# Moving one bank copy ahead, keeping the last gated chunks on the chip, and moving the residual loads to GpSimd's queue, in a float32 gated block

## The chip, the cores and the metric

The kernel runs on one core of one Trainium2 chip. The core has five engines that work in parallel: TensorE (PE: matmuls, into PSUM banks of 128 x 512 float32), VectorE (DVE), ScalarE (ACT), GpSimd (POOL) and SyncE (SP), which here only issues DMAs. SP, ACT and POOL each issue DMAs on a queue of their own. Each engine runs its instructions in order and waits on semaphores for the others. The metric is the time of one execution on the device in microseconds (us).

## The reference

A residual block on x of 1024 tokens by 1024 channels, in float32. Its second half is a gated feed-forward layer, and its first step is one wide input projection:

```python
h = rms_norm(x, norm_mix_g[l]) * (1.0 + sc1) + sh1
proj = jnp.einsum('bsd,de->bse', h, w_in[l])          # 7 x 1024 columns
...
x = x + g1 * mix
h2 = rms_norm(x, norm_ffn_g[l]) * (1.0 + sc2) + sh2
a, bgate = jnp.split(jnp.einsum('bsd,df->bsf', h2, w_ffn_in[l]), 2, axis=-1)
x = x + g2 * jnp.einsum('bsf,fd->bsd', jax.nn.silu(a) * bgate, w_ffn_out[l])   # 2816 hidden channels
return rms_norm(x, final_norm_g)
```

Between them lie two convolution mixers, their projections and a gated merge, which the change does not touch.

## The kernel before

Everything is held transposed, channels on the 128 partitions and tokens along the free axis, so x is 8 tiles of 128 x 1024 and the hidden layer 22 chunks (f = 0 to 21). Tokens are used in two halves of 512, which is one PSUM bank.

**Matmuls.** A float32 operand is split in a high part (a cast on ScalarE: `wh`, `th`) and a low part (the difference, on VectorE or GpSimd: `wl`, `tl`). `mm3` multiplies them in three matmuls: wh by th (L323), wh by tl (L324), wl by th (L326). A row "L324 x<-tl,wh" is thus the second matmul of a triple into a bank of x, and it needs the low part.

**Duals and products.** Matrix products are done in pairs of column blocks, called duals, by a scheme with seven products in place of eight, named "1", "2", "6", "5", "7", "3", "4" in the order they run. Sums of blocks of the weights (L243 to L245, L259, on 128 x 1024 or 128 x 768 tiles called `raw`) are made beforehand. "1", "6", "7" and "4" use the two banks x (one for each of the two column blocks, p = 0 and 1), "2" the banks y, "5" and "3" the banks z. A product that uses a bank again adds to what stands in it, and may start only when the intermediate sum has been read. A product of an input dual has 2 x 4 triples, one of an output dual 2 x 3.

**Run-ahead.** For the first duals of the input projection the products "1" and "2" are computed early, while the normalisation of the second token half is still being made. Their results are kept in tiles `m1`. `win_dual` (L760) copies `m1` back into the two banks x at the head of each such dual, and "6" then adds to them. The loop `steps` (L637 on) is the last part of the run-ahead; its last pass computes product "2" of the last of these duals.

**Feed-forward input.** Eleven duals (d = 0 to 10) make two hidden chunks each. `hid_set(d)` prepares them as operands: for d = 0 to 8 the seven combinations that the output duals use, for d = 9 and 10 (chunks 18 to 21, from `REST` on) the plain chunks. `store` splits a tile into a high and a low half in one of three buffers called `stage`, and GpSimd's queue writes it to DRAM (L1166, 512 KB). `t_load` (L1192) reads it back in two halves of 256 KB, `th` and `tl`, into tiles of a pool of 58.

**Feed-forward output.** Three groups g of three pairs of chunks, in two duals d of the output channels each: (0,0), (0,1), (1,0) and so on. `product` runs the seven products, and after each `out_evac` (L1263) adds the bank to the residual tiles x1 (x10 to x17) in place on VectorE: "1", "2", "6" and "3" to x10 and x11 in dual d = 0 (x12 and x13 in d = 1), "5", "7" and "4" to x14 and x15 (x16 and x17). x10 and x11 are loaded early; the other six are loads of 512 KB on SP's queue (L1256), in the order 4, 5, 2, 3, 6, 7, into a pool `x1b` opened when the pools `gi` and `stage` are closed, in their memory. The products of a group are loaded one group ahead. Chunks 18 to 21 are multiplied last, in pieces of tokens, followed by the final normalisation.

**What sets the order.** The program is written in one sequence; a scheduler with its own simulated times orders each engine's instructions, and pools of buffers add waits. `tc.issue_after(ins)` keeps what is issued under it behind `ins` on the same engine only. GpSimd's DMAs use eight semaphores in turn, so each waits until the one eight before it has landed.

Of the kernel before, what the change touches and what calls it, by code (L numbers as in the profile page):

```python
# [45 lines left out]
FC = DFF // P  # L46
# [59 lines left out]
REST = 2 * GROUP * GROUPS  # L106
# [9 lines left out]
def block_kernel(ctx: ExitStack, tc: tile.TileContext, xt, x0, xT, c, vecs, ada, w_first, w_duals,  # L116
# [522 lines left out]
    for i, (d, m) in enumerate(steps):  # L639
        if 0 < i <= KH:  # L640
            h1_pair(i - 1)
        w = next_w()
        for p in range(d == LEAD // 2, 2):
            if m == "1":
                ahead[d, p] = ps_tile("ahead")
            for k in range(KH):
                c0 = ((p * KH if d > LEAD // 2 else 0) + k) * P
                mm3([ahead[d, p]], slice(c0, c0 + P), w, [th[m][k]], m == "1" and k == 0, k == KH - 1, m == "2")
            (m1_store if m == "1" else first_out)(d, p, ahead[d, p])
        if i == 0:  # L650
            with tc.issue_after(mm3.ins):
                rx_1 = row_sum(spread)
# [60 lines left out]
    def win_dual(d, pairs, x, y, z):  # L713
# [44 lines left out]
        if d < AHEAD_DUALS:  # L758
            for p in range(2):
                nc.scalar.copy(x[p], m1[d, p])  # L760
# [121 lines left out]
    n_duals = len(PAIRS) // 2  # L882
    banks = [[ps_tile(b) for _ in range(2)] for b in "xyz"]
    for d in range(n_duals):
# [273 lines left out]

    hid_dram = {}

# [7 lines left out]
    def hid_set(d):  # L1168

        (b11, b12), (b21, b22) = ((ha[2 * d + p, "4"], ha[2 * d + p, "6"]) for p in range(2))  # L1170
        if 2 * d >= REST:
            for p, half in enumerate(((b11, b12), (b21, b22))):
                for h in range(2):
                    store((2 * d + p, h), half[h])
            return
# [78 lines left out]
    x1 += [x1bp.tile([P, T], F32, tag="x1", name=f"x1{j}") for j in range(2, KC)]  # L1254
    for j in (4, 5, 2, 3, 6, 7):
        nc.sync.dma_start(x1[j], x1_dram[j])  # L1256

# [9 lines left out]

    hid = {}
    n = 2 * GROUP * P
# [4 lines left out]
    for g in range(GROUPS):  # L1274
        for d in range(2):
            banks = {}
            for m in PRODUCTS:
                product(banks, m, to[g, m], out_evac(d))
                if d == 0 and m == "1":
                    if g < GROUPS - 1:  # L1280
                        for q in PRODUCTS:
                            group_load(g + 1, q)
                    else:
                        for h in range(2):
                            for f in range(REST, FC):
                                hid[f, h] = t_load((f, h))
# [166 lines left out]
```

## Time and profile before

| | |
|---|---|
| median of 3 runs | 1468.57 us (1468.46 to 1469.9) |
| the profiled execution | 1469.82 us |
| its span, first to last instruction | 1468.0 us |
| mean granted clock of TensorE | 0.996 |
| DMA | 262.98 MB, mean 179 GB/s |

The profile is of one execution. A row of the waits reads: engine, what it waited to do, the line, what released it, total us, times, longest. A row of a timeline reads: start, us, engine, line, operation, tile written <- tiles read, count, and in brackets the idle time before it and what ended that. A row of the windows gives the stretch, then for PE, PEld, DVE, ACT and POOL the busy time with the number of instructions, then the granted clock, the share of DMA and GB/s. SPq is SyncE's queue of DMA issues. The last number of a DMA row is the median time from issue to landing.

The input projection's first dual starts near 88 us. The last feed-forward input dual ends and the output phase begins near 1236 us.

### The profile page before, as it was taken

To read this page: it belongs to the slowest core of one execution; us is meant where nothing else is said; L and a number is where in the kernel's file an instruction comes from. 1 tells how busy PE (TensorE), PEld (TensorE's weight loads), DVE (VectorE), ACT (ScalarE), POOL (GpSimd) and SP (SyncE) were. 2 spreads that over 40 slices of the span, in tenths; PEclk is the share of its full clock that TensorE was granted. 3 is DMA by queue.
4 is the path that set the end of the run, shared out by engine and by line. 5 is a ranking of instruction groups with operands and counts; after the bars stand their busy time and mean duration, and the time that the engine had idled before them with its cause. 6 is when DMAs were issued, how large, how long until landed. Compare 5 with 4: busy or idle time off the path is not lost.

```text
span 1468.0 us, 17816 instructions
## 1 busy us (share of the span) xinstructions
PE 1447.8 (99%) x6393; PEld 1188.4 (81%) x6393; DVE 1167.9 (80%) x1604; ACT 652.7 (44%) x959; POOL 527.4 (36%) x466
## 2 busy tenths in 40 slices
PE   8999999999999999999999999999999999999997
PEld 4778888888888888888888888888888888788887
DVE  6898899999989959999677897677776665676755
ACT  4874443433333446465236565444444443122235
POOL 0028788768777762111022002001011025435105
PEclk9999999999999999999999999999999999999999
DMA  9943554231322346576485348454554459998403
GB/s 380 363 157 117 178 158 129 87 129 59 128 86 73 113 145 220 196 231 204 147 287 187 104 155 274 143 181 167 171 178 148 144 176 375 343 282 269 143 22 115
DMA packets 90618, 262.98 MB, mean 179 GB/s; under 512 B 10401, under 2 KB 12577, under 8 KB 90530
## 3 DMA queue, kind: packets, MB, share of 16 engines
q1 hardware_dynamic: 45952, 149.97, 30.7%
q0 software_dynamic: 37232, 96.49, 20.1%
q10 hardware_dynamic: 7346, 15.40, 2.8%
q8 instruction: 50, 0.82, 0.2%
q14 instruction: 38, 0.31, 0.1%
HBM read 198.90 MB, written 62.91 MB: 178 GB/s over the span
## 4 chain that ended last, share of the span: by engine, by line
PE 51%; issue 4%; DVE 2%; DMA 1%; POOL 1%; ACT 0%; POOLq 0%; DVEq 0%; SPq 0%
PE x L323 8%; PE x L324 8%; PE x L326 8%; PE z L323 4%; PE z L326 4%; PE z L324 4%; PE y L323 3%; PE y L326 3%; PE y L324 3%; PE mix L323 2%; PE mix L326 2%; PE mix L324 2%; PE yb L323 1%; PE yb L324 1%; PE yb L326 1%
## 5 line engine op out<-in xcount | busy, mean ns | idle before, releaser
L220 ACT CAST wh<-raw 128x1024 fp32r<-128x1024 f32 (+3 forms) x262 | 264.6, 1011 | 412.2 <-PE x L324 117.1
L221 DVE TENSOR_TENSOR wl<-raw,wh 128x1024 fp32r<-128x1024 f32 (+2 forms) x180 | 208.5, 1160 | 75.6 <-ACT wh L220 74.2
L221 POOL TENSOR_TENSOR wl<-raw,wh 128x1024 fp32r<-128x1024 f32 x82 | 202.0, 2469 | 90.2 <-ACT wh L220 90.2
L821 DVE SCALAR_TENSOR_TENSOR c<-diff,vec,c 128x512 f32<-128x512 f32 x248 | 179.0, 750 | 2.7
L1166 POOL DMA_DIRECT2D hid<-stage x71 | 37.8, 533 | 336.8 <-DVE stage L364 333.9
L324 PE MATMUL x<-tl,wh 128*128 128x512 f32 x304 | 118.6, 390 | 0.6 <-DVE tl L364 0.6
L323 PE MATMUL x<-th,wh 128*128 128x512 f32 x304 | 118.5, 390 | 0.0
L326 PE MATMUL x<-th,wl 128*128 128x512 f32 x304 | 118.3, 389 | 0.0
L323 PE MATMUL z<-th,wh 128*128 128x512 f32 x216 | 84.6, 392 | 2.1 <-DVE x L1263 2.1
L821 DVE SCALAR_TENSOR_TENSOR c<-u,wsum,c 128x512 f32<-128x512 f32 x112 | 84.1, 751 | 2.0
L326 PE MATMUL z<-th,wl 128*128 128x512 f32 x216 | 84.5, 391 | 0.0
L324 PE MATMUL z<-tl,wh 128*128 128x512 f32 x216 | 84.5, 391 | 0.0
L326 PE MATMUL y<-th,wl 128*128 128x512 f32 x180 | 70.1, 390 | 0.2 <-POOL wl L221 0.2
L324 PE MATMUL y<-tl,wh 128*128 128x512 f32 x180 | 70.0, 389 | 0.0
L323 PE MATMUL y<-th,wh 128*128 128x512 f32 x180 | 70.0, 389 | 0.0
L364 DVE TENSOR_TENSOR stage<-g,stage 128x512 fp32r<-128x512 f32 x62 | 41.9, 688 | 34.5 <-ACT stage L363 34.5
L243 POOL TENSOR_TENSOR raw<-raw 128x1024 f32<-128x1024 f32 x13 | 33.6, 2582 | 95.3 <-DVE t2l L364 78.9
L324 PEld LDWEIGHTS x<-tl,wh 128*128 128x128 f32 x304 | 57.2, 188 | 12.9 <-DVE tl L364 1.0
L323 PEld LDWEIGHTS x<-th,wh 128*128 128x128 f32 x304 | 57.2, 188 | 12.0
L326 PEld LDWEIGHTS x<-th,wl 128*128 128x128 f32 x304 | 57.2, 188 | 11.8
L1192 POOL DMA_DIRECT2D th<-hid x71 | 38.2, 538 | 75.2 <-PE x L326 56.6
L363 ACT CAST stage<-g 128x512 fp32r<-128x512 f32 x62 | 37.4, 619 | 51.8 <-DMA hid<-stage 43.5
(759 smaller groups left out, 4023.4 us busy)
## 6 DMA issues: line engine op xcount, KB each, us to landing
hid<-stage POOLq DMA_DIRECT2D x71, 512.0 KB, 5.2
raw<-in_w_duals SPq DMA_DIRECT2D x66, 512.0 KB, 3.6
raw<-in_w_fi SPq DMA_DIRECT2D x53, 512.0 KB, 4.6
th<-hid POOLq DMA_DIRECT2D x71, 256.0 KB, 5.7
tl<-hid POOLq DMA_DIRECT2D x71, 256.0 KB, 5.8
ada<-in_ada SPq DMA_DIRECT2D x33, 512.0 KB, 6.0
raw<-in_w_fo SPq DMA_DIRECT2D x24, 384.0 KB, 6.5
raw<-in_w_conf SPq DMA_DIRECT2D x16, 512.0 KB, 4.3
```

Of the source, the lines that this page charges most:

```text
L220: hi = nc.scalar.copy(wh, raw)
L221: lo = lo_engine.tensor_tensor(wl, raw, f32(wh), ALU.subtract)
L243: eng.tensor_tensor(a["s1"], a["21"], a["22"], ALU.add)
L323: nc.tensor.matmul(ps, wh, xh, start=first, stop=False, skip_group_check=again)
L324: nc.tensor.matmul(ps, wh, xl, start=False, stop=False, skip_group_check=again)
L326: mm3.ins = nc.tensor.matmul(ps, wl, xh, start=False, stop=last, skip_group_check=again).ins
L363: nc.scalar.copy(hi, src)
L364: t_split.ins = nc.vector.tensor_tensor(lo, src, f32(hi), ALU.subtract).ins
L821: tap.ins = nc.vector.scalar_tensor_tensor(out=out, in0=src[:, s : s + H], scalar=wt, in1=acc, op0=ALU.mult, op1=ALU.add).ins
L1166: nc.gpsimd.dma_start(hid_dram[key], s)
L1192: nc.gpsimd.dma_start(t, hid_dram[key][:, s])
```

## The change

It has two parts.

**The copy.** The copy of the first dual's first bank from `m1[0, 0]` is no longer made at the head of `win_dual`; it is issued in the last pass of `steps`, ahead of that pass's matmuls, into a bank taken there. The second bank is copied where it was.

**The last chunks and the residual.** For the last input dual (chunks 20 and 21) `hid_set` splits straight into tiles of the pool of 58 (`hid`), which stay until the end; they are neither stored nor loaded again. Chunks 18 and 19 go by DRAM as before. The six residual loads are issued on GpSimd's queue, in two calls: x14 and x15 where the six stood, the other four after the first output product.

```diff
         w = next_w()
+        if i == len(steps) - 1:
+            first_x = [ps_tile("x")]
+            nc.scalar.copy(first_x[0], m1[0, 0])
         for p in range(d == LEAD // 2, 2):
...
         if d < AHEAD_DUALS:
-            for p in range(2):
+            for p in range(d == 0, 2):
                 nc.scalar.copy(x[p], m1[d, p])
...
-    banks = [[ps_tile(b) for _ in range(2)] for b in "xyz"]
+    banks = [first_x + [ps_tile("x")]] + [[ps_tile(b) for _ in range(2)] for b in "yz"]
...
-    hid_dram = {}
+    hid_dram, hid = {}, {}
...
                 for h in range(2):
-                    store((2 * d + p, h), half[h])
+                    if d < N_IN - 1:
+                        store((2 * d + p, h), half[h])
+                    else:
+                        hid[2 * d + p, h] = t_pair("hid")
+                        t_split(half[h], *hid[2 * d + p, h])
...
-    for j in (4, 5, 2, 3, 6, 7):
-        nc.sync.dma_start(x1[j], x1_dram[j])
+
+    def x1_load(js):
+        for j in js:
+            nc.gpsimd.dma_start(x1[j], x1_dram[j])
+
+    x1_load((4, 5))
...
                 product(banks, m, to[g, m], out_evac(d))
+                if (g, d, m) == (0, 0, "1"):
+                    with tc.issue_after(mm3.ins):
+                        x1_load((2, 3, 6, 7))
...
-                            for f in range(REST, FC):
+                            for f in range(REST, FC - 2):
                                 hid[f, h] = t_load((f, h))
```

The scheduler's order changes in three places.

ScalarE at the end of the run-ahead, before and after. `x_915` (after: `x_808`) is the first bank x of the first dual, `x_916` (`x_917`) the second; `ahead` are the run-ahead's banks, `th` the high parts of the operands for "5" and "7".

```order
L582 COPY p2_820<-ahead_689 128x512
L363 CAST th_838<-x00_213 128x512
L586 ACTIVATE sig_835<-ahead_706 128x512
L760 COPY x_915<-m1_332 128x512
L587 DMA gate_a0_118<-sig_835 128x512
L363 CAST th_842<-x10_227 128x512
L760 COPY x_916<-m1_337 128x512
```

```order
L645 COPY x_808<-m1_332 128x512
L582 COPY p2_822<-ahead_689 128x512
L586 ACTIVATE sig_837<-ahead_706 128x512
L363 CAST th_840<-x00_213 128x512
L587 DMA gate_a0_118<-sig_837 128x512
L363 CAST th_844<-x10_227 128x512
L763 COPY x_917<-m1_337 128x512
```

The first copy has moved ahead of three instructions, the second stands where it was. On TensorE the three matmuls of "5" that read `th_840` and `tl_841` now stand between the two halves of "6".

VectorE some 10 us further on, before and after. `wl_963` is the low part of the weights of product "3"; `tl_859`, `tl_863`, `tl_867` (after: `tl_861`, `tl_865`, `tl_869`) are low parts of the second, third and fourth chunk of product "7".

```order
L364 TENSOR_TENSOR tl_859<-x11_497,th_858 128x512
L364 TENSOR_TENSOR tl_863<-x21_499,th_862 128x512
L221 TENSOR_TENSOR wl_963<-raw_959,wh_962 128x1024
L364 TENSOR_TENSOR tl_867<-x31_501,th_866 128x512
L364 TENSOR_TENSOR tl_871<-x41_503,th_870 128x512
```

```order
L364 TENSOR_TENSOR tl_861<-x11_497,th_860 128x512
L221 TENSOR_TENSOR wl_963<-raw_959,wh_962 128x1024
L364 TENSOR_TENSOR tl_865<-x21_499,th_864 128x512
L364 TENSOR_TENSOR tl_869<-x31_501,th_868 128x512
L364 TENSOR_TENSOR tl_873<-x41_503,th_872 128x512
```

The weights' split has moved ahead of the third chunk's. ScalarE's casts for it moved in the same way: the second bank's copy `v_953` and the cast `wh_962` stand one or two places sooner.

GpSimd's queue at the start of the output phase, before and after. `hid20_0` to `hid21_1` are the stores that go away, `hid3_1` and so on the loads of the second group, `x14` to `x17` and `x12`, `x13` the residual.

```order
L1192 DMA tl_9883<-hid2_4_7658 128x512
L1166 DMA hid20_0_9889<-stage_9886 128x1024
L1166 DMA hid20_1_9894<-stage_9891 128x1024
L1166 DMA hid21_0_9899<-stage_9896 128x1024
L1192 DMA th_9977<-hid3_1_7908 128x512
L1166 DMA hid21_1_9904<-stage_9901 128x1024
L1192 DMA tl_9978<-hid3_1_7908 128x512
L1192 DMA th_9981<-hid4_1_8193 128x512
```

```order
L1199 DMA tl_9883<-hid2_4_7658 128x512
L1199 DMA th_9973<-hid3_1_7908 128x512
L1265 DMA x14_9917<-x1_dram4_5925 128x1024
L1265 DMA x15_9918<-x1_dram5_5926 128x1024
L1265 DMA x12_9915<-x1_dram2_5923 128x1024
L1265 DMA x13_9916<-x1_dram3_5924 128x1024
L1265 DMA x16_9919<-x1_dram6_5927 128x1024
L1265 DMA x17_9920<-x1_dram7_5928 128x1024
L1199 DMA tl_9974<-hid3_1_7908 128x512
```

The stores are gone, and all six residual loads stand together, one place behind the first store's old place: `issue_after` a matmul holds nothing back on GpSimd.

VectorE in the first output dual, after, where the additions of "5" and "7" to x14 and x15 stand. `z` holds "5", `x` holds "7"; `wl_10135` is the low part of the weights of "4"; `raw_10162` is a block of the weights of dual (0,1).

```order
L221 TENSOR_TENSOR wl_10109<-raw_9925,wh_10108 128x768
L1274 SCALAR_TENSOR_TENSOR x14_9917<-z_10112,ng2_9902,x14_9917 128x512
L1274 SCALAR_TENSOR_TENSOR x15_9918<-z_10123,ng2_9902,x15_9918 128x512
L221 TENSOR_TENSOR wl_10135<-raw_9929,wh_10134 128x768
L243 TENSOR_TENSOR raw_10214<-raw_10162,raw_10164 128x768
L1274 SCALAR_TENSOR_TENSOR x14_9917<-x_9947,ng2_9902,x14_9917 128x512
L244 TENSOR_TENSOR raw_10162<-raw_10162,raw_10158 128x768
L1274 SCALAR_TENSOR_TENSOR x15_9918<-x_9958,ng2_9902,x15_9918 128x512
```

Before, the three sums L243 to L245 stood six instructions later, behind the next dual's first two weights. SP issues the load of `raw_10162` when `wl_10109` is done; before, the corresponding load stood behind the six residual loads.

More of the change, by code (lines that the diff above doesn't have):

```diff
@@ L1266, in out_evac @@
         return evac
-    hid = {}
     n = 2 * GROUP * P
```

## The prediction

> **What bounds the kernel now.** I read the page's engine shares first, then the waits of TensorE, then the two places where the change acts. Times are us from the span's start.
>
> ```profile
> PE 1447.8 (99%) x6393; PEld 1188.4 (81%) x6393; DVE 1167.9 (80%) x1604; ACT 652.7 (44%) x959; POOL 527.4 (36%) x466
> PE z L323 <- DVE x L1263: 2.1, 1, 2.1
> ...
> PE x L323 <- ACT x L760: 1.4, 1, 1.4
> ...
> PE x L324 <- DVE tl L364: 0.6, 1, 0.6
> ```
>
> TensorE is busy for 99% of the span, so an edit can only win back a stall of TensorE. The first two waits are the two that the change aims at; the third lies 14 us behind the second and is fed by the same engines.
>
> The larger one stands in the output phase. Four windows of equal length, and TensorE's events around the stall:
>
> ```profile
> 1200.00:1240.00 40.00, 40.00 (x178) 33.15 (x177) 22.44 (x28) 16.18 (x25) 24.05 (x46) 1.00 1.08 338
> 1240.00:1280.00 40.00, 37.87 (x160) 30.81 (x160) 23.87 (x32) 7.80 (x10) 16.77 (x33) 0.96 1.06 351
> ...
> 1257.95 0.39 PE L326 MATMUL z<-th,wl 128*128 128x512 f32 x1
> 1260.47 0.50 PE L323 MATMUL z<-th,wh 128*128 128x512 f32 x1 [2.13 <-DVE x L1263]
> ...
> 1263.38 0.63 PE L326 MATMUL z<-th,wl 128*128 128x512 f32 x1
> 1263.80 0.63 PE L323 MATMUL x<-th,wh 128*128 128x512 f32 x1
> ...
> 1262.00:1263.00 1.00, 1.00 (x4) 0.71 (x4) 1.00 (x2) 0.00 (x0) 0.00 (x0) 0.50 1.11 399
> ```
>
> The second window holds 160 matmuls where the first holds 178. At 40 / 178 = 0.225 us each, 18 missing ones are 4.05 us. Only 2.3 us of that is the gap (1258.18, one step after the last matmul, to 1260.47); the rest is the slow stretch behind it, in which the granted clock is 0.50 and matmuls start 0.42 us apart instead of 0.227.
>
> What TensorE waited for:
>
> ```profile
> SPq L1256 <- DMA hid<-stage: 8.2, 1, 8.2
> ...
> 1253.29 6.25 DMA x<-x_dram
> 1259.66 0.76 DVE x L1263
> ```
>
> The bank of product "3", second half, still held product "5"; VectorE could not add it to x15 because x15 had not landed. Its load stood in SP's queue for 8.2 us behind the landing of a store from the stage buffers, whose memory x15 takes over.
>
> The second place is the start of the first dual:
>
> ```profile
> 87.78 0.39 PE L326 MATMUL ahead<-h70h,wl 128*128 128x512 f32 x1
> 89.58 0.50 PE L323 MATMUL x<-t2h,wh 128*128 128x512 f32 x1 [1.42 <-ACT x L760]
> ...
> 86.50 1.04 ACT L220 CAST wh<-raw 128x1024 fp32r<-128x1024 f32 x1
> ...
> 88.92 0.60 ACT L760 COPY x<-m 128x512 f32<-128x512 f32 x1
> ```
>
> The next slot was 88.01, the matmul came at 89.58: 1.57 us lost, on a ScalarE copy that stood behind three others.
>
> **Part B, the on-chip hidden chunks and the residual loads.** Removed: four stores of 512 KB, eight loads of 256 KB, and the wait of x15 for a store's landing. The four splits write other tiles at the same price: no change on ScalarE or VectorE, except that the ScalarE split which waited for a stage buffer does not wait. Moved: six loads of 512 KB from SP's queue to GpSimd's, where they stand one place behind the old place of the first store:
>
> ```profile
> 1239.13 0.54 POOL L1166 DMA_DIRECT2D hid<-stage  x1 [0.15 <-issue]
> 1239.81 1.17 POOL L1166 DMA_DIRECT2D hid<-stage  x2
> ...
> hid<-stage POOLq DMA_DIRECT2D x2, 512.0 KB, 8.0
> th<-hid POOLq DMA_DIRECT2D x9, 256.0 KB, 8.3
> ```
>
> x14 and x15 now take the slots 1239.81 and about 1240.45. The two stores issued there, of the same size on the same queue, landed after 8.0 us at the median. So I put x14 and x15 at about 1248 and 1249. They are wanted by 1255.4 (x14, to be added before the first half of product "3", which starts nine matmuls, 2.04 us, before 1258.18) and by 1257.4 (x15). That is over 7 us to spare, and the stall goes: -4.05. The other four loads are wanted from 1266 on and issued by 1243. Beyond 1257.4 each us late costs one, and at 1259.6, 19 us after issue, nothing is gained. Ends: 0 and -4.05; the row is far nearer to the second.
>
> What is late next? Two things.
>
> First, VectorE's queue: the sum L243 of the next weights now stands behind `wl_10135` and ahead of the second addition to x14. It waits for `raw_10162`, which SP issues when `wl_10109` is done:
>
> ```profile
> 1249.59 0.95 DVE L221 TENSOR_TENSOR wl<-raw,wh 128x768 fp32r<-128x768 f32 x1
> ...
> raw<-in_w_fo SPq DMA_DIRECT2D x24, 384.0 KB, 6.5
> ...
> raw<-in_w_fo SPq DMA_DIRECT2D x2, 384.0 KB, 14.5
> ```
>
> Issue 1250.5, landing 6.5 later at 1257.0, sum 0.95, addition 0.75: the bank is free at 1258.7. Product "4" wants it at 1258.18 + 2.04 = 1260.2. Slack 1.5 us, so I take 0 for it. The other end is the 14.5 us of the second row, seen when that load stood behind five residual loads in SP's own queue: free at 1266.7, a stall of 6.5 us. Now the residual loads are on the other queue and mostly landed by 1252, so the median is the nearer row.
>
> Second, the eight tiles that keep the hidden chunks leave 50 of 58 for the streamed loads, so loads for the second group wait until the second dual of the first group frees tiles, from about 1266. They are read from about 1293 (seven products of 18 matmuls from 1264.3). With 8.3 us for a load, nothing there reaches TensorE; 0. GpSimd issues no arithmetic in this phase, so nothing but these loads is queued behind its waits.
>
> **Part A, the copy.** x[0] is now copied in front of the `p2` copy, behind the cast that ends at 87.54: 87.44 to 88.03, and TensorE starts at 88.09, 1.49 us sooner. The copies and casts it passes are each 0.6 later by that, and still ahead of their readers. The lead does not last. The order puts the first three matmuls of product "5" ahead of the second half of "6". Twelve matmuls from 88.09 end the first half at 90.9; the next but one wants a low part that VectorE ends at 91.26 (first of the three from 90.59) and waits 0.2. Fifteen more matmuls start by 94.5: "6" ends near 94.65, 0.67 sooner than before (95.31, where ScalarE's copy `v` follows at 95.35). The 21 left of "5" bring "7" to 99.24, where it was 100.59. It wants the low parts of its third and fourth chunk seven and ten matmuls later, at 100.83 and 101.5. They come so:
>
> ```profile
> 97.27 2.41 POOL L244 TENSOR_TENSOR raw<-raw 128x1024 f32<-128x1024 f32 x1 [12.37 <-DMA raw<-in_w_duals]
> 99.76 3.27 POOL L245 TENSOR_TENSOR raw<-raw 128x1024 f32<-128x1024 f32 x1
> ...
> 90.59 1.88 DVE L364 TENSOR_TENSOR tl<-x,th 128x512 fp32r<-128x512 f32 x3
> 92.39 1.21 DVE L221 TENSOR_TENSOR wl<-raw,wh 128x1024 fp32r<-128x1024 f32 x1
> ...
> 96.49 0.69 DVE L364 TENSOR_TENSOR tl<-x,th 128x512 fp32r<-128x512 f32 x1 [1.08 <-ACT th L363]
> 97.44 3.33 DVE L221 TENSOR_TENSOR wl<-raw,wh 128x1024 fp32r<-128x1024 f32 x1 [0.26 <-ACT wh L220]
> 100.68 4.11 DVE L364 TENSOR_TENSOR tl<-x,th 128x512 fp32r<-128x512 f32 x3
> ...
> 95.35 0.59 ACT L772 COPY v<-x 128x512 f32<-128x512 f32 x1 [1.10 <-PE x L326]
> ...
> 96.35 1.05 ACT L220 CAST wh<-raw 128x1024 fp32r<-128x1024 f32 x1
> ...
> 103.64 0.50 PE L324 MATMUL x<-tl,wh 128*128 128x512 f32 x1 [0.62 <-DVE tl L364]
> ```
>
> A split that takes 1.21 took 3.33 while GpSimd's sum ran, and of the three behind it (0.69 when free) the first took 2.9: the two engines shut each other out. After the change the third chunk's `tl_865` stands behind `wl_963`, not ahead of it. ScalarE's chain of v, th and wh (2.05 us, 95.35 to 97.40 before) now runs from 94.68, so `wl_963` starts at 96.78; GpSimd's data lands at 97.27 as before, so it waits for the split's end at 98.0. [...]
>
> If GpSimd goes first: sum to 100.4, `tl_865` done at 100.9 (0.1 late), second sum to 103.2, `tl_869` done at 103.75. TensorE goes on at 103.79 against 103.64 before: all 1.49 us are gone, +0.15. If VectorE goes first, both low parts are there by 101.5, and up to 103.64 - 101.5 = 2.1 us stay; a sum of GpSimd's then falls among the splits for product "3" and may take 0.9 of it back (-1.2 to -2.1, middle -1.6). The rows lean to the first:
>
> ```profile
> 531.09 2.84 POOL L259 TENSOR_TENSOR raw<-raw 128x1024 f32<-128x1024 f32 x1
> 533.89 2.84 POOL L221 TENSOR_TENSOR wl<-raw,wh 128x1024 fp32r<-128x1024 f32 x1
> ...
> 531.60 6.29 DVE L710 TENSOR_TENSOR q<-sc,q 128x512 f32<-128x512 f32 x3
> ...
> 80.94 3.96 POOL L243 TENSOR_TENSOR raw<-raw 128x1024 f32<-128x1024 f32 x1 [78.94 <-DVE t2l L364]
> ...
> 81.97 0.68 DVE L627 TENSOR_TENSOR x<-x,x 128x512 f32<-128x512 f32 x1
> ```
>
> At 99.76, 531.09 and 533.89 GpSimd was waiting and went ahead of the next VectorE instruction; at 80.94 it waited, and VectorE's next, at 81.97, still went first. I take +0.15, between ends of -2.1 and +1.9 (below).
>
> [...]
>
> **Sum.** -4.05 + 0.15 = -3.9. On the profiled execution's 1469.82 that is 1465.9. That execution stands 1.25 above the median of the three runs, 1468.57, and the comparison is of medians: 1464.7.
>
> **The rivals.**
> [...]
> - The new stall of "7" is a gap of 2.1 us, as long as the one at 1260.47, and brings the slow clock with it: 1.75 more (4.05 - 2.3). For it: that row. Against: the 1.42 gap at 89.58 had no slow matmuls behind it, and 2.13 is the shortest here that did. -4.05 + 1.9 = -2.15, so 1466.4.
> - Part B doesn't do what it says: x14 or x15 lands late, behind eight outstanding loads with the queues at 351 GB/s, and half of the stall stays. For it: the loads of 10 us and more around 1255. Against: even 14.5 us would be in time. -2 + 0.15 = -1.85, so 1466.7.
> - The slow stretch from 1261 on is not brought by the gap and stays when the gap closes. For it: the 1.42 gap had no such stretch. Against: no other stretch of 1240 to 1280 is slow, and this one follows the gap. -2.3 + 0.15 = -2.15, again 1466.4. [...]
> - Slower: `raw_10162` lands late and VectorE, in order, holds the additions behind L243. Above a landing at 1258.5 each us costs one, and a gap of 2 us brings the slow clock's 1.75. It ends over 0.2% slower from a stall of 5.1 us on, a landing at 1263.6, 13.1 us after issue. For it: the 14.5 row, which gives -4.05 + 6.5 + 1.75 + 0.15 = +4.35, so 1472.9. Against: it stood behind five loads then.
>
> **How the numbers follow.** 0.2% is 2.9 us, about what a measurement of this kernel can tell from no change: faster is below 1465.6, slower above 1471.5. Chances: forecast 0.29, VectorE first 0.21, slow clock in "7" 0.19, half stall 0.14, slow stretch stays 0.05, late L243 0.12 (0.10 of it slower, 0.02 same). Faster 0.29 + 0.21 = 0.50, slower 0.10, same 0.40. The range goes from 1462.4 (VectorE first at its end of -2.1) to 1468.6, which takes in the half stall together with the slow clock in "7" (-2 + 1.9); it leaves out the late L243 and little below. The forecast with VectorE first, the faster cases alone, is 1462.4 to 1465.5.
>
> **What the profile after would show.** TensorE's wait on DVE x in the output phase gone, and 178 matmuls in 1240 to 1280; x14 and x15 landed by 1250; no TensorE wait on L1274 near 1260. In the first dual TensorE's x at 88.1 without the ScalarE wait, and in its place a wait of L324 on `tl` of about 2 us near 101.6, with GpSimd's L244 starting its work as VectorE's `wl` ends. The prediction is wrong if `wl` and both `tl` run back to back there, if the clock falls behind that wait, or if L243 stands idle on a load beyond 1258.5.

## The result, and the profile after

The changed kernel takes 1467.20 us at the median of 20 runs (1464.4 to 1469.39); the kernel before, run beside it, takes 1470.14 (20 runs, 1467.77 to 1474.14). That is 2.94 us less, a ratio of 0.998 with a 95% interval of 0.9973 to 0.9987. It is faster by about the 0.2% that a measurement of this kernel can tell from no change. The prediction had a saving of 3.9 us and put it against a median of three runs, 1468.57, which lay 1.57 below the later one.

The profiled execution of after took 1468.79 us (span 1467.0, mean granted clock 0.996), so it is only 1.0 shorter than the one before, and that 1.0 is a sum of terms of both signs. TensorE's longest waits, in the view of the waits of the changed kernel:

```profile
PE x L324 <- DVE tl L364: 1.8, 1, 1.8
PE lead L485 <- POOL idle L478: 1.7, 1, 1.7
PE lead L323 <- ACT m L556: 1.5, 1, 1.5
PE y L326 <- POOL wl L221: 0.6, 1, 0.6
PE z L323 <- DVE ma L686: 0.5, 1, 0.5
```

The wait on x of the output phase (2.1 before) and the wait for ScalarE's copy (1.4) are gone. The wait of product "7" for a low part, 0.6 before, is now 1.8 and stands first.

The output phase, from the windows, TensorE's timeline and VectorE's timeline of after:

```profile
1200.00:1240.00 40.00, 40.00 (x178) 33.13 (x177) 19.71 (x24) 15.58 (x23) 20.53 (x39) 1.00 0.96 300
1240.00:1280.00 40.00, 40.00 (x178) 33.11 (x177) 29.58 (x40) 10.24 (x15) 17.61 (x34) 1.00 0.89 292
```

```profile
1263.37 0.39 PE L323 MATMUL x<-th,wh 128*128 128x512 f32 x1
```

```profile
1253.37 0.75 DVE L1274 SCALAR_TENSOR_TENSOR x<-z,ng,x 128x512 f32<-128x512 f32 x1 [0.40 <-PE z L326]
...
1259.94 0.96 DVE L243 TENSOR_TENSOR raw<-raw 128x768 f32<-128x768 f32 x1 [2.88 <-DMA raw<-in_w_fo]
1260.81 0.75 DVE L1274 SCALAR_TENSOR_TENSOR x<-x,ng,x 128x512 f32<-128x512 f32 x1
```

178 matmuls stand in the second window, where there were 160, and the clock there is 1.00. VectorE's sum L243 sat idle for 2.88 on its load, as was feared, but the addition behind it ended at 1261.56 and product "4" started at 1263.37 without a wait: 1.8 us to spare. The residual loads, from the DMA view of 1244.2 to 1245:

```profile
x<-x_dram POOLq DMA_DIRECT2D x2, 512.0 KB, 7.1
```

The first dual, from the windows and TensorE's timeline, and from VectorE's and GpSimd's timelines:

```profile
80.00:120.00 40.00, 38.18 (x160) 30.68 (x159) 36.30 (x40) 26.26 (x44) 16.59 (x8) 0.96 0.35 111
...
106.00:108.00 2.00, 2.00 (x7) 1.62 (x6) 2.00 (x4) 0.00 (x0) 0.00 (x0) 0.62 0.00 0
108.00:110.00 2.00, 2.00 (x6) 1.52 (x6) 1.87 (x4) 1.14 (x2) 0.00 (x0) 0.53 0.77 199
110.00:112.00 2.00, 2.00 (x11) 1.61 (x10) 1.57 (x3) 1.89 (x3) 0.76 (x1) 1.00 0.16 64
```

```profile
89.50 0.39 PE L326 MATMUL ahead<-h70h,wl 128*128 128x512 f32 x1
89.73 0.39 PE L323 MATMUL x<-t2h,wh 128*128 128x512 f32 x1
...
102.97 0.40 PE L323 MATMUL x<-th,wh 128*128 128x512 f32 x1
105.18 0.50 PE L324 MATMUL x<-tl,wh 128*128 128x512 f32 x1 [1.82 <-DVE tl L364]
```

```profile
98.30 1.23 DVE L221 TENSOR_TENSOR wl<-raw,wh 128x1024 fp32r<-128x1024 f32 x1 [0.25 <-ACT wh L220]
99.45 6.88 DVE L364 TENSOR_TENSOR tl<-x,th 128x512 fp32r<-128x512 f32 x4
```

```profile
98.75 3.04 POOL L244 TENSOR_TENSOR raw<-raw 128x1024 f32<-128x1024 f32 x1 [12.46 <-DMA raw<-in_w_duals]
101.87 2.71 POOL L245 TENSOR_TENSOR raw<-raw 128x1024 f32<-128x1024 f32 x1
```

TensorE goes from the run-ahead's last matmul into the first dual in one step, 0.23 us. Then GpSimd's two sums get in between VectorE's splits, four of which take 6.88 (the first two 2.9 each, where one takes 0.69 when free); the gap at 102.97 is 1.99 us (105.18 less one step of 0.227), and the clock falls to 0.53 behind it.

The two profiled executions, matmul by matmul (6393 in each):

| stretch of TensorE | before | after | difference |
|---|---|---|---|
| start to the run-ahead's last matmul | 87.78 | 89.50 | +1.73 |
| from there to the first matmul of product "4" of the first dual | 24.61 | 26.06 | +1.45 |
| from there to the output phase | | | -0.02 |
| 100 matmuls around the old stall | 26.73 | 22.67 | -4.06 |

They add up to -0.9, against -1.0 of the spans. The first row is not the change's: the code there is the same, and behind a gap at 38.5 that both have, only this execution shows a slow clock:

```profile
40.00:45.00 5.00, 4.47 (x12) 3.22 (x13) 4.96 (x8) 4.07 (x9) 0.00 (x0) 0.66 0.98 368
```

In the kernels below the run-ahead ends between 87.8 and 89.5 as well, at 89.2 or later only in those whose profile has a slow clock behind this gap. So in the table that follows a stretch is always measured from the run-ahead's last matmul.

### The profile page after: what moved, and what is told of

The parts are those of the page before. It is cut to its first block, busy times and chain, and to the rows that moved or that the text cites. A ratio compares the mean times of both kernels' runs of the same rounds, so it can differ in the third digit from the quotient of the medians.

```text
span 1467.0 us, 17767 instructions
## 1 busy us (share of the span) xinstructions
PE 1451.6 (99%) x6393; PEld 1190.7 (81%) x6393; DVE 1169.3 (80%) x1604; ACT 652.8 (44%) x959; POOL 524.3 (36%) x460
## 4 chain that ended last, share of the span: by engine, by line
PE 83%; DVE 10%; DMA 4%; issue 2%; ACT 1%; POOL 1%; SPq 0%; POOLq 0%; ACTq 0%; DVEq 0%
PE x L324 11%; PE x L326 10%; PE x L323 10%; PE z L323 7%; PE z L326 7%; PE z L324 7%; PE y L323 6%; PE y L324 6%; PE y L326 6%; DVE c L824 3%; PE yb L323 2%; PE mix L326 2%; PE yb L326 2%; PE mix L324 2%; PE mix L323 2%; PE yb L324 2%
## 5 line engine op out<-in xcount | busy, mean ns | idle before, releaser
L243 POOL TENSOR_TENSOR raw<-raw 128x1024 f32<-128x1024 f32 x13 | 33.4, 2570 | 97.4 <-DVE t2l L364 80.4
L304 DVE CUSTOM_DVE_ANT_0 ada<-ada,cs,vec 128x1024 f32<-128x1024 f32 x33 | 50.3, 1540 | 8.0 <-DMA ada<-in_ada 7.3
```

The lines of the kernel that those rows point to most:

```text
L243: eng.tensor_tensor(a["s1"], a["21"], a["22"], ALU.add)
L304: modulation.ins = nc.vector.tensor_tensor_reduce(out=raw, in0=raw, in1=cs, scale=1.0, scalar=col(V_ADA, b), op0=ALU.mult, op1=ALU.add, ac ...
```

## The experiments

My theory was the prediction's: the four stores' memory held x15 back, and leaving them out closes the stall; the early copy gains 1.5 us that are lost again where VectorE's splits stretch beside GpSimd's sums (before, one of 1.21 us took 3.33), with or without the slow clock. The rivals: VectorE goes first and the copy gains; the queue, not the stores, was the cause of the stall; the slow stretch in the output phase does not belong to the gap.

The kernels, each against runs of the kernel before on the same chip. "First dual" is the second stretch of the table above, "output" the 100 matmuls around the stall; both are of one profiled execution. "Lead" is how far TensorE stands from the kernel before (negative is ahead), from the run-ahead's last matmul on, at the end of the first dual (behind product "4", so it can differ from the difference of the first column), at about 700 us, and behind the output stall.

| kernel | ratio (95%) | median, against before | first dual | output | lead |
|---|---|---|---|---|---|
| before | | | 24.61 | 26.73 | 0 / 0 / 0 |
| the change | 0.998 (0.9973 to 0.9987) | 1467.20, 1470.14 | 26.06 | 22.67 | +1.45 / +1.43 / -2.64 |
| copy_alone | 1.0006 (0.9995 to 1.0016) | 1471.09, 1470.91 | 23.63 | 25.01 | -0.58 / +0.92 / -0.81 |
| chunks_alone | 0.9976 (0.9965 to 0.9987) | 1467.23, 1470.91 | 23.86 | 22.67 | -0.75 / +0.59 / -3.49 |
| split_held | 0.9968 (0.9957 to 0.9979) | 1465.33, 1470.91 | 22.59 | 22.67 | -1.59 / +0.88 / -3.05 |
| chunk_last | 0.9981 (0.9971 to 0.9991) | 1467.54, 1470.91 | 24.74 | 22.67 | +0.13 / +0.91 / -3.19 |
| chunks_sp | 0.9973 (0.9963 to 0.9982) | 1466.17, 1470.12 | 24.55 | 22.67 | -0.07 / +0.65 / -3.43 |
| queue_alone | 0.9982 (0.9973 to 0.9991) | 1468.11, 1470.12 | 23.82 | 24.61 | -0.79 / -1.48 / -3.59 |
| chunks_held | 0.9963 (0.995 to 0.9975) | 1465.64, 1470.12 | 23.75 | 22.67 | -0.87 / -1.12 / -5.19 |
| copy_later | 1.0027 (1.0018 to 1.0036) | 1474.44, 1470.12 | 29.27 | 27.06 | +4.65 / +4.56 / +4.88 |
| sp_held | 0.9964 (0.9952 to 0.9975) | 1464.74, 1470.05 | 23.73 | 22.67 | -0.88 / -1.25 / -5.33 |
| sp_held_copy | 0.9961 (0.9949 to 0.9972) | 1464.37, 1470.05 | 22.66 | 22.67 | -1.33 / -1.43 / -5.50 |
| taps_held | 0.9983 (0.9974 to 0.9992) | 1467.56, 1470.05 | 23.75 | 22.67 | -0.86 / +0.25 / -3.82 |
| taps_held_copy | 0.998 (0.997 to 0.999) | 1466.38, 1470.05 | 22.20 | 22.67 | -1.93 / -0.45 / -4.51 |

### copy_alone: the kernel before with the early copy only

```diff
+        if i == len(steps) - 1:
+            first_x = [ps_tile("x")]
+            nc.scalar.copy(first_x[0], m1[0, 0])
...
-            for p in range(2):
+            for p in range(d == 0, 2):
                 nc.scalar.copy(x[p], m1[d, p])
```

> The kernel before with the copy alone. The stretch is measured on TensorE from the last matmul of the run-ahead to the first of product "4" of the first dual: 24.61 us before, 26.06 after the whole change. If the copy turns into a later stall of product "7" (a wait of L324 on tl of about 1.8 us, with GpSimd's sums between VectorE's splits), the stretch here is 26.1 where the slow clock follows the stall and 24.7 where it doesn't, and the time is 0 to 1.5 us above before. If the loss seen in the changed kernel came from another part of the change or from chance, the wait is not here and the stretch is 22.5 to 23.2, 1.4 to 2.1 us faster than before. The wait in the output phase stays at 2.1 us.

Measured: 1.0006, no change that can be told. The profile shows the other order of the two engines. GpSimd's and VectorE's timelines:

```profile
98.82 2.72 POOL L244 TENSOR_TENSOR raw<-raw 128x1024 f32<-128x1024 f32 x1 [13.38 <-DMA raw<-in_w_duals]
```

```profile
97.47 1.23 DVE L221 TENSOR_TENSOR wl<-raw,wh 128x1024 fp32r<-128x1024 f32 x1 [0.25 <-ACT wh L220]
98.61 6.90 DVE L364 TENSOR_TENSOR tl<-x,th 128x512 fp32r<-128x512 f32 x4
```

Here the run-ahead's last matmul is at 88.18, so GpSimd's sum begins 10.64 us behind it, against 9.25 in the kernel with the whole change (98.75 - 89.50), and the third chunk's split, at 98.61, is ahead of it. From the span's start the two sums begin at the same time (98.82 and 98.75); it is VectorE's weights' split that stands later in the changed kernel's profile (98.30 for 97.47), as its run-ahead ended 1.3 later, behind the slow clock near 42. Product "7" has no wait, and the first dual is 0.98 shorter than before: the outcome with VectorE first, though 23.63 lies between the two cases that I had set. All of that is given back before 700 us, 0.4 of it in product "4" and the rest at other waits (1.0 for a low part of GpSimd's in y, 0.8 on VectorE's `ma`, against 0.7 for the second before). So the order of the two engines does decide what happens in the first dual, but even where it goes well the copy alone is worth nothing that shows in the time.

This kernel still has the stall of the output phase. Its timeline and window there:

```profile
1259.27 0.39 PE L326 MATMUL z<-th,wl 128*128 128x512 f32 x1
1261.70 0.50 PE L323 MATMUL z<-th,wh 128*128 128x512 f32 x1 [2.04 <-DVE x L1266]
```

```profile
1240.00:1280.00 40.00, 37.96 (x168) 31.08 (x166) 24.61 (x34) 8.14 (x11) 18.06 (x35) 1.00 1.10 366
```

The gap is 2.20 us, 0.09 less than before, and no slow clock follows: 168 matmuls, not 160, at 1.00. The same stall cost 4.06 us in one execution and 2.34 (25.01 less 22.67) in this one.

### chunks_alone: the change without the early copy

```diff
-        if i == len(steps) - 1:
-            first_x = [ps_tile("x")]
-            nc.scalar.copy(first_x[0], m1[0, 0])
...
-            for p in range(d == 0, 2):
+            for p in range(2):
                 nc.scalar.copy(x[p], m1[d, p])
```

> The changed kernel with both copies back at the head of the first dual. If the two parts act independently, the wait of TensorE on x in the output phase is gone, the output phase wins 4.07 us as in the changed kernel, the wait on the copy (1.4) and the one on tl (0.6) are back, and the time is 4.0 us below before and about 1 us below the changed kernel. If part of the gain comes from the copy, or if the additions behind the sum L243 wait for their load in some executions, the gain is 2 to 3 us.

Measured: 0.9976, 3.7 us by the medians, as good as the whole change or better. The output stretch is the same 22.67. The second part of the change carries the gain.

The first dual is 0.75 shorter than before, although its code and the order of its instructions are those of before. VectorE's and GpSimd's timelines:

```profile
97.79 1.23 DVE L221 TENSOR_TENSOR wl<-raw,wh 128x1024 fp32r<-128x1024 f32 x1 [0.26 <-ACT wh L220]
```

```profile
97.88 3.39 POOL L244 TENSOR_TENSOR raw<-raw 128x1024 f32<-128x1024 f32 x1 [12.63 <-DMA raw<-in_w_duals]
```

The split starts 0.09 ahead of GpSimd's sum and takes 1.23; in the profile before it started 0.17 behind it (97.44 and 97.27) and took 3.33. So the wait on `tl` that I expected to be back (0.6) is not there. queue_alone has the split first too (97.79 and 98.04, first dual 23.82); chunks_sp has it 0.01 behind the sum (98.92 and 98.91), where it takes 3.48 and TensorE waits 0.8. Some 0.7 us of the first dual thus hang on which of the two starts first, by 0.25 us at most, without any edit there. And copy_alone's 23.63 is only 0.2 less than what the code of before does when the split comes first.

### split_held: the change, with the weights' split held behind product "7"

`t_split` notes its two instructions, and in the first dual the split of product "3"'s weights is issued behind the last of the low parts for "7".

```diff
+        if m == "7":
+            hold += [t_split.act, t_split.ins]
...
-            w = split_w(a[...], n, (), los)
+            w = split_w(a[...], n, hold if first and m == "3" else (), los)
```

> The whole change, with the split of product "3"'s weights in the first dual held behind the low part of product "7"'s last chunk, on ScalarE and VectorE. If the place of that split in front of the two low parts is what made them late, the wait of L324 on tl is gone, the stretch from the last run-ahead matmul to product "4" is 22.5 to 23.0 us (26.06 in the changed kernel, 24.61 before) and the time is 5.5 to 6 us below before. If GpSimd's sums shut VectorE out wherever the split stands, the stall moves to product "3", whose weights then come late, and the stretch stays at 24.5 or more.

Measured: 0.9968. VectorE's timeline and the window of the first dual:

```profile
96.16 1.90 DVE L364 TENSOR_TENSOR tl<-x,th 128x512 fp32r<-128x512 f32 x3 [1.20 <-ACT th L363]
98.14 3.25 DVE L221 TENSOR_TENSOR wl<-raw,wh 128x1024 fp32r<-128x1024 f32 x1
```

```profile
80.00:120.00 40.00, 39.88 (x174) 31.97 (x173) 36.33 (x40) 27.96 (x46) 19.70 (x9) 1.00 0.39 117
```

All three low parts are made by 98.1, though GpSimd's first sum starts at 97.59, and it is the weights' split, which nobody waits for yet, that takes 3.25 in place of 1.2. TensorE does 174 matmuls in the window where the change does 160; the first dual is 22.59, 3.5 us shorter than with the change. So the 1.8 us wait is due to the place of the weights' split among VectorE's instructions. The time shows 2.6 of it by the medians (5.6 less than before, against 2.9), and the two ratios' intervals overlap.

### chunk_last: the change, with product "7" doing the first three chunks of both banks before the fourth

```diff
+            late = KH - 1 if (d, m) == (0, "7") else 0
+            for p in range(2 if late else 0):
+                for k in range(late):
+                    c0 = (p * KH + k) * P
+                    mm3([banks[m][p]], slice(c0, c0 + P), w, [th[m][k]], False, False, True)
             for p in range(2):
...
-                for k in range(KH):
+                for k in range(late, KH):
```

> The whole change, with product "7" of the first dual doing the first three chunks of both banks before the fourth of either, so that nine matmuls (2.04 us) stand where TensorE waited for the fourth low part. VectorE and GpSimd work in the same order as in the changed kernel, and the low part is as late. If the loss is the stall and the slow clock behind it, both go: the wait is at most 0.3 us, no matmul after it is slow, and the stretch is 22.7 to 23.5 us (26.06 in the changed kernel), the time 5 to 5.5 us below before. If VectorE and GpSimd are behind as a whole, the stall moves to product "3" and the stretch is 24 us or more.

Measured: 0.9981, as the change. The wait did not go away; it moved to product "3", whose low parts stand behind four that took 6.92 us beside the same sums of GpSimd's. TensorE's timeline:

```profile
110.89 0.50 PE L324 MATMUL z<-tl,wh 128*128 128x512 f32 x1 [1.81 <-DVE tl L364]
```

The gap is 1.98 us, as long as the change's 1.99, and no slow clock follows it (1.00 from 110 to 116); the first dual is 1.32 shorter than the change's for that reason. To wait later is no cure, VectorE's queue has to be shorter ahead of what TensorE wants.

### chunks_sp: the chunks stay on the chip, the residual loads stay on SP's queue, no early copy

Against chunks_alone:

```diff
-            nc.gpsimd.dma_start(x1[j], x1_dram[j])
+            nc.sync.dma_start(x1[j], x1_dram[j])
 
-    x1_load((4, 5))
+    x1_load((4, 5, 2, 3, 6, 7))
...
-                if (g, d, m) == (0, 0, "1"):
-                    with tc.issue_after(mm3.ins):
-                        x1_load((2, 3, 6, 7))
```

> The kernel before with the last chunks kept on the chip alone: the six residual loads stay on SP's queue, in one call, and the copy is as before. If the stall of the output phase came from x15's memory waiting for the last stores from the stage buffers, leaving out the stores is enough: SP's wait of 8.2 us is gone, x14 and x15 land by 1253, TensorE does not wait on x, and the time is 3 to 4 us below before, as with the chunks and GpSimd's queue together (0.9976). If the move to GpSimd's queue is needed, x14 and x15 come behind SP's other loads, a wait of 1 us or more stays, and the time is within 2 us of before.

Measured: 0.9973, 22.67 in the output stretch, no wait on x. The longest wait of SP's queue for a landing there, in the view of the waits:

```profile
SPq L1262 <- DMA tl<-hid: 0.7, 2, 0.5
```

The 8.2 us behind the landing of a store are gone although the loads stand on the queue they always stood on; x15 landed at 1255.19, 2 us later than I expected, and early enough. Leaving out the stores is enough.

### queue_alone: the kernel before with the residual loads on GpSimd's queue

```diff
     for j in (4, 5, 2, 3, 6, 7):
-        nc.sync.dma_start(x1[j], x1_dram[j])
+        nc.gpsimd.dma_start(x1[j], x1_dram[j])
```

> The kernel before with the six residual loads moved to GpSimd's queue alone; the stores stay. If the memory of the stage buffers is the cause, x15 still waits for the landing of the last store, now on GpSimd's queue with the loads of the second group behind it; the wait of TensorE on x stays at 2 us or grows, and the time is 0 to 3 us above before. If SP's queue was the cause, the wait goes and the time is 3 to 4 us below before.

Measured: 0.9982, about 2 us less than before, where I had expected no gain or a loss. TensorE's timeline:

```profile
1254.67 0.39 PE L326 MATMUL x<-th,wl 128*128 128x512 f32 x1
1256.40 0.47 PE L323 MATMUL z<-th,wh 128*128 128x512 f32 x1 [1.34 <-ACT wh L220]
```

VectorE's, where the wait comes from (the row above names ScalarE, which had long been done):

```profile
1255.55 0.75 DVE L1263 SCALAR_TENSOR_TENSOR x<-z,ng,x 128x512 f32<-128x512 f32 x1 [6.15 <-DMA x<-x_dram]
```

A stall stays, now on x14, of 1.5 us (1256.40 - 1254.67, less one step) and with no slow clock (the matmuls behind it start 0.23 us apart at the median). x14's load stands on GpSimd's queue behind the last store and is issued at 1248.08, 4.9 later than before. GpSimd's queue still waits 2.2 us for a store to land before it may load x15, but the last store lands after 4.4 us in this execution. So the move of the queue by itself shortens the stall and does not close it. Together with chunks_sp: the stores were the cause, and the move of the loads is not needed once they are gone.

### copy_later: the kernel before with the first bank copied four times

```diff
             for p in range(2):
-                nc.scalar.copy(x[p], m1[d, p])
+                for _ in range(1 if d or p else 4):
+                    nc.scalar.copy(x[p], m1[d, p])
```

> The kernel before with the first bank copied four times over, so that TensorE starts the first dual about 3 us later than before. If the time to about 620 us is set by VectorE and GpSimd, a part of the delay is made up: TensorE's waits on GpSimd's split near 221 and on VectorE near 617 (0.2 and 0.7 in the profile before, up to 1.3 and 1.1 in the kernels that were ahead) are the shorter, and the time is 1 to 2 us above before. If TensorE sets the time throughout, the whole 3 us remain.

Measured: 1.0027, 4.3 us slower. From TensorE's timeline and the windows:

```profile
88.88 0.39 PE L326 MATMUL ahead<-h70h,wl 128*128 128x512 f32 x1
93.94 0.79 PE L323 MATMUL x<-t2h,wh 128*128 128x512 f32 x1 [4.67 <-ACT x L761]
```

```profile
92.00:96.00 4.00, 2.06 (x5) 1.68 (x6) 3.51 (x6) 4.00 (x8) 0.00 (x0) 0.51 0.34 123
96.00:100.00 4.00, 4.00 (x14) 3.11 (x13) 3.23 (x5) 2.72 (x6) 0.00 (x0) 0.64 0.21 70
```

I had expected 3 us. The gap is 3.25 longer than before, and the slow clock behind it, which I had left out, takes another 2.3; with the wait at "7" gone, 4.65 remain. This delay of 4.65 us at the end of the first dual is still 4.56 at 700 us and 4.88 behind the output phase. What TensorE loses here is lost for good. That makes it stranger that what it gains in copy_alone is not kept.

### chunks_held, sp_held and sp_held_copy: the held split without the copy, and the best of the parts together

chunks_held is chunks_alone with the held split; sp_held is chunks_sp with it; sp_held_copy is sp_held with the early copy as well.

```diff
-            w = split_w(a[...], n, (), los)
+            w = split_w(a[...], n, hold if first and m == "3" else (), los)
```

> The held split together with the chunks and loads of the change, but without the early copy. If the held split is what makes split_held (0.9968) better than the whole change (0.998), and the early copy gives nothing that lasts, this one is as fast as split_held, 4 to 5 us below before. If the early copy's 1.5 us last once the low parts come in time, this one is 1.5 us slower than split_held.

> The kernel before with the last chunks kept on the chip (residual on SP's queue, as in chunks_sp) and the held split, without the early copy: the smallest edit that holds what the runs so far showed to help. If the two gains add, 0.9973 from the chunks and about 0.8 us from the held split, the time is 4.5 to 5.5 us below before, as chunks_held (0.9963). If GpSimd's queue was needed for the second part of chunks_held's gain, it is 3.5 to 4 us.

> sp_held with the early copy. If a lead of TensorE in the first dual is eaten again by the waits on VectorE, ScalarE and GpSimd between 220 and 620, where VectorE is busy for 57 to 59 of 60 us, TensorE is 0.7 to 2 us ahead of sp_held at the end of the first dual and 0.5 us or less ahead at 700, and the times are within 0.5 us. If the lead lasts, this one is 1 to 2 us faster than sp_held.

Measured: 0.9963, 0.9964 and 0.9961. The windows of sp_held_copy:

```profile
80.00:120.00 40.00, 39.82 (x173) 31.72 (x172) 36.32 (x40) 28.01 (x46) 19.39 (x9) 1.00 0.40 117
1240.00:1280.00 40.00, 40.00 (x178) 33.12 (x177) 27.75 (x36) 8.29 (x10) 13.12 (x25) 1.00 0.90 298
```

Both stalls are closed in one kernel, 5.7 us less than before by the medians, and this is the lowest median against before of all, though no run tells it from sp_held or chunks_held. The copy's share of it is 0.4 us, which no run here can tell from nothing; the queue of the residual loads makes no difference that shows (0.9963 and 0.9964). In all three profiles the first dual is free of the wait for a low part, and in all three its lead is still there at 700 us. Without the copy, though, the held split doesn't make the first dual shorter than chunks_alone's and queue_alone's (23.75 and 23.73 against 23.86 and 23.82); it makes sure of what these two got without it. What it is worth in time there, 0.8 and 1.4 us by the medians, lies within the intervals.

### taps_held and taps_held_copy: is it VectorE's load that eats the lead?

The leads of copy_alone, chunks_alone and split_held are gone by 700 us, in the part of the program where the convolution's taps keep VectorE busy for 55 to 59 of every 60 us (180 to 480, before). These two are sp_held and sp_held_copy with six of the 46 taps of each channel block left out, so that this part of the sum is missing from the result.

```diff
-        for s in range(CK // 2 + 1):
+        for s in range(CK // 2 + 1 - 6):
             tap(a0, d, s, col(V_CW + 2 * s * KC, j), a0)
```

> sp_held with six of the 46 taps of each channel block of the long convolution left out (the last six of its third loop), which are 48 instructions of 0.75 us on VectorE between 150 and 480. It serves as the base of taps_held_copy. If VectorE's load is what TensorE waits for at 220 to 620, the waits there, 2 to 3 us in sum in the kernels that were ahead, shrink to 1 us or less and the time is 1 to 2 us below sp_held. If they are set by the order of a few instructions, nothing changes by more than 0.5 us.

> taps_held with the early copy; the same six taps are left out. If VectorE's load eats the lead, it lasts here: TensorE is 0.7 to 2 us ahead of taps_held at the end of the first dual, still ahead by that at 700, and the time is lower by that. If something else eats it, the two times are within 0.5 us, as sp_held and sp_held_copy.

Measured: 0.9983 and 0.998. From the groups by line of sp_held and of taps_held, the taps:

```profile
L823 DVE SCALAR_TENSOR_TENSOR c<-diff,vec,c 128x512 f32<-128x512 f32 x248 | 178.9, 749 | 2.7
```

```profile
L823 DVE SCALAR_TENSOR_TENSOR c<-diff,vec,c 128x512 f32<-128x512 f32 x200 | 143.9, 750 | 2.4
```

and from the waits of taps_held:

```profile
PE z L323 <- DVE ma L685: 1.7, 1, 1.7
...
PE y L326 <- POOL wl L221: 1.2, 1, 1.2
```

VectorE has 35 us less to do, and taps_held is 2.8 us slower than sp_held by the medians: the waits near 617 and 221 grow, from 0.6 and 0.4. What I expected of taps_held failed. For taps_held_copy the first case came out, narrowly: it is 1.07 ahead of taps_held at the end of the first dual and 0.70 at 700, and its median is 1.2 lower, which can't be told from nothing with runs that spread over 4 to 5 us. Against the kernel before both lose their lead by 700 us, by 1.1 and 1.5 us. So a VectorE with less to do did not keep a lead. Without the six taps the scheduler's order is the same on TensorE and GpSimd, but other in a few dozen rows on ScalarE, VectorE and SyncE's queue; the runs don't say whether that is what made the waits grow.

## Why the prediction came out as it did

**The direction and the size.** The forecast, 3.9 us less, lies just inside the interval (0.9973 is 3.97 us, 0.9987 is 1.9); the measured 2.94 is 1 us short of it. Faster was the likelier side and the time is in the range. Of the time itself less should be made: 1467.20 is 2.5 above the 1464.7 that was forecast, and 1.57 of that is the low median of three runs that it was reckoned from.

**What the profile was to show.** The wait on x, the 178 matmuls, the start of the first dual without a wait and the wait of "7" behind L244 came as said. But two of the three things by which the prediction was to be wrong came too. The clock fell behind that wait, which is a term that the sum had put at nothing and a rival had at 0.19. And L243 stood idle on a load that landed at 1259.86, beyond 1258.5; this one is a shift, for TensorE was 3.2 us later there than before (1.73 + 1.43), and product "4" did not wait. x14 and x15 landed at 1250.57 and 1252.82, not by 1250: they were issued 4.5 and 4.4 later than the slots that were read off (1244.34 and 1244.86), for the same 3.2 and for loads that GpSimd's queue waited on.

**Part B, -4.05: the mechanism right, the size that of one execution.** In the pair of profiled executions the stall gave -4.06. But -1.75 of the term is the slow clock behind the gap, and copy_alone has nearly the same gap (2.20 for 2.29) without it. copy_later has the stall a third time, with a gap of 2.92 and the slow clock (27.06, 4.4 over 22.67). So the stall cost 2.3 in one of these executions and 4.1 or more in two, and the prediction set what one execution showed, "18 missing ones are 4.05 us", against medians. As an average that may still hold: chunks_alone gives 3.7 us and chunks_sp 4.0 by the medians, with intervals of 1.9 to 5.1 and 2.6 to 5.4. Which term the missing 1 us belongs to is not shown by the times; copy_alone alone has anything from -0.7 to +2.4 for the first part.

**The cause of the stall: right.** chunks_sp shows that leaving out the stores closes it, with the loads where they were. queue_alone shows that the move of the queue shortens it without closing it. The two loads took 6.2 and 8.0 us to land (7.1 at the median), where 8.0 was taken.

**The late load in VectorE's queue: right.** The weights' load was put at 6.5 us and took 6.86 (1253.00 to 1259.86); the slack was put at 1.5 us and was 1.8. The rival that would have made the kernel slower had no part in it.

**The rival that the slow stretch is not brought by the gap: right in one half.** copy_alone shows a gap without the stretch; no kernel without the gap shows the stretch there. In these runs a gap was needed and not enough.

**Part A, +0.15: the mechanism right, the slow clock left out.** The order of the two engines came as forecast: in the changed kernel's profile GpSimd's sum, idle for 12.46 us on its load, is ahead of the low parts behind the weights' split, and the first two of these took 2.9 us each in place of 0.69, at a price of 1.99 us. The lead won was 1.6 (forecast 1.49) and the loss at "7" was 2.99 (1.64): the gap of 1.99 and 1.8 of the slow clock behind it, less the 0.8 lost at that place before. That is the mechanism of the rival with the slow clock in "7", put at +1.9 and measured at +1.45 in this one execution. In copy_alone the outcome with VectorE first came, and the time did not follow; that outcome came not because VectorE went ahead while both waited, but because GpSimd's data came later against VectorE's queue. The prediction put the data 0.49 behind the start of the weights' split (97.27 and 96.78); it was 0.45 in the changed kernel's profile and 1.35 in copy_alone's, long enough for a low part to come between. Which case an execution gets goes, in these profiles, by which engine starts first, as chunks_alone and chunks_sp show with unchanged code (the split 0.09 ahead of the sum takes 1.23 us, 0.01 behind it 3.48). The sum of parts is thus better written as a mean: about -3.5 to -4 for the second part, and for the first something between nothing and +1.

**What stays open.** Where TensorE's leads of under 2 us from the first dual are lost before 700 us. They are lost in copy_alone, chunks_alone, split_held and the two kernels without the six taps (by 1.1 to 2.5 us) and kept in chunks_held, sp_held and sp_held_copy (within 0.4) and in queue_alone, which has no held split. The profiles are one each, and they differ by as much from one execution to the next: the waits near 221 and 617 are up to 1.3 and 1.1 long, and the second is missing in queue_alone, without any edit there. That VectorE's load is the reason is not borne out by taps_held, but the changed order keeps it from being ruled out; a chance of the executions would do, and was not tested.

## What to carry to other kernels

When a kernel is bound by TensorE at 99%, price a stall by the gap in its timeline and put the slow stretch behind it as a second term with a chance of its own, since the next execution may not have it (here 6 of 26 gaps of 1.5 to 2.3 us had it). A buffer whose last use is a store delays whoever inherits its memory until that store has landed (SP's queue stood for 8.2 us here); leaving the store out left no stall, where moving the load to another queue left one of 1.5 us. And where an engine's instructions stretch beside another's (a weights' split of 1.2 us on VectorE took 3.25 to 3.48 beside a sum of GpSimd's), it pays to look at which instruction stands in the way and is not urgent: to hold one weights' split back by 1.5 us closed the stall that starting the stretch 1.6 us sooner had brought. And before a difference of under 1 us between two profiles is put down to an edit, look for kernels that have the same code there: the first dual read 23.82 to 24.61 with none.

## What the runs showed of the hardware that was not expected

The clock falls behind gaps of 1.65 to 2.3 us in some executions only. From 20 us on TensorE has 26 gaps of 1.5 to 2.3 us over the 14 profiles (from one matmul's start to the next, less one step); behind 6 of them the next 22 matmuls lost 1.4 us or more, behind 20 they lost 0.6 or less. The 6 are at 1257.95 before (2.29), at 38.5 and 102.97 after (1.65 and 1.99), and near 37.8 in chunk_last, chunks_sp and taps_held_copy (2.20, 2.21 and 2.22); chunks_alone has 2.30 near 37.8 with no slow clock behind it. The two longer gaps, both in copy_later (2.92 and 4.83), were followed by it. So a gap of 1.65 us was followed by it in one execution and one of 2.30 was not in another; what decides it is not shown.

A kernel with 35 us less work on VectorE was slower by the medians, 0.9983 against 0.9964 (the intervals meet at 0.9974 and 0.9975). The order changed with it on three engines, so which of the two did it is open.
